# Weights of the seven-product units begin 64 bytes into places that grow by 256 bytes

## The chip, the cores and the metric

The kernel runs on one core of a Trainium2 chip. Five engines work side by side on one on-chip memory of 128 partitions (SBUF): TensorE (PE, with its weight loads shown apart as PEld), VectorE (DVE), ScalarE (ACT), GpSimd (POOL) and SyncE (SP), and DMA queues bring weights in from DRAM. The metric is the device time of one execution in microseconds. Of the kernel before it is 1582.96 us, the median of three runs from 1582.42 to 1583.38.

## The reference

One layer of a decoder trunk: a SwiGLU block, a mixer of two gated linear recurrences, and a second SwiGLU block, for 512 tokens of width 1024, in float32.

```python
D_MODEL = 1024
SEQ = 512
D_FF = 2816

def swiglu(x, w_in, w_out):
    a, b = jnp.split(x @ w_in, 2, axis=-1)
    return (jax.nn.silu(a) * b) @ w_out
...
        h = h + 0.5 * swiglu(rmsnorm(h, ffn1_norm[l]), ffn1_w_in[l], ffn1_w_out[l])
        h = h + hybrid_mixer(rmsnorm(h, mix_norm[l]), w_in[l], lb_all[l], hgrn_out_norm[l],
                             gdn_conv_w[l], gdn_a_log[l], gdn_dt_bias[l], gdn_out_norm[l],
                             w_branch_hgrn[l], w_branch_gdn[l], w_out[l])
        h = h + 0.5 * swiglu(rmsnorm(h, ffn2_norm[l]), ffn2_w_in[l], ffn2_w_out[l])
    return rmsnorm(h, final_norm)
```

The change lies in the products `x @ w_in` of both SwiGLU blocks. Each is a product of a 512 by 1024 matrix with a 1024 by 5632 one.

## The kernel before

**Products in three parts.** Every large product is made of two-part numbers. A weight tile of 128 x 512 is brought into SBUF in float32, ScalarE rounds it into a tile `whi` of the type float32r, and VectorE subtracts to get the rest, `wlo`. The other operand has such a pair, too (`uh`, `ul`, or slices of `xs`). `mm3` (lines 193 to 196) then issues three matmuls: high by high, high by low, low by high. Each matmul has a stationary operand of 128 x 128, which a weight load (LDWEIGHTS) of its own brings into the array, and a moving operand, whose columns stream through. The load of one matmul runs beside the matmul ahead of it.

**Places for weights.** `pair` (line 177) hands out the tiles `wlo` and `whi`. There are two lanes, `w` and `v`, with WB // 2 = 3 places for each of the two tiles, so 12 places of 128 x 512 numbers in all, 2,048 bytes in each partition. The built program puts the first at byte 72,704 of a partition, a multiple of 512, and the others right behind it, so each begins at a multiple of 512. All users of weights share these places: the plain units, the mixer's slabs, and the units below. In SBUF the mixer's tiles and those of the two SwiGLU blocks lie behind them. The operands `uh`, `ul` and `xs` begin at multiples of 512, too.

**Seven-product units.** In a SwiGLU block, `ffn` walks over 22 groups of 2 x 128 columns of `w_in`. The first few are taken as plain products (`plain`), the others by `fast` (line 358), which replaces eight block products by seven products of sums and differences of blocks. There are 17 such groups in the first block and 19 in the second. One group makes seven `Unit`s, each with four blocks of 128 rows, and for each of these `mm3` with 256 columns: 36 x 7 x 4 x 3 = 3024 matmuls, which the profile names px. `xs` holds the seven moving operands. A unit's weight is a loaded tile (`rw`) or a sum or difference of such tiles (`sw`, made by VectorE in line 370).

**Order.** `stream` (line 286) runs through all units of a block in a fixed order. Behind each unit's matmuls, `ahead` prepares weights of later units, up to LEAD = 9 ahead: it asks `pair` for two tiles in the unit's lane, ScalarE writes `whi` (line 333), and VectorE writes `wlo` (line 312). A unit that has a `fold` gets its `wlo` another way: ScalarE writes `-whi` into it (line 337), and a DMA from the POOL queue adds the raw weight from DRAM to that (line 338).

**The other stages.** The blocks' second products (`w_out`) and the mixer use matmuls of 512 columns (pmm, pnat). In pnat the weights are the moving operand, in pmm the stationary one. The order of all instructions is written out by the program, in the mixer by the planner `Desk`.

Of the kernel before, what the change touches and what calls it, by code (L numbers as in the profile page):

```python
# [9 lines left out]
F32R = mybir.dt.float32r  # L10
# [6 lines left out]
P = 128  # L17
# [22 lines left out]
WB = 6  # L40
# [14 lines left out]
LAG = dict(raw=3.5, gb=6.5, nb=6, m=7, out=5.5, back=6, turn=5.5)  # L55
EASE = 2.5
TURNED = (0, 1)
LANES = {"a": 2, "b": 2, "d": 1, "e": 1}


# [85 lines left out]
def body(tc, xT, cst, sqc, hmask, dta, w1o, w1a, w2a, wt, wn, wab, wbh, wbg, wo, w1b, w2b, gfin, y, dbg=None):  # L146
# [4 lines left out]
    wp = ctx.enter_context(tc.tile_pool(name="wp", bufs=1))  # L151
# [22 lines left out]

    taken = [0]

    def pair(lane=None):

        taken[0] += 1
        n = "wv"[taken[0] % 2 if lane is None else lane]  # L180
        return [wp.tile([P, 512], F32R, tag=n + x, name="w" + x, bufs=WB // 2) for x in ("lo", "hi")]

    def slab(src):
        f = src.shape[-1]
# [73 lines left out]
    class Raw:  # L258

        def __init__(self, src, readers=1, fast=False):  # L260
            self.src, self.left, self.fast = src, readers, fast

    class Unit:

        def __init__(self, raws, operand, run, comb=None, drop=(), fold=None, lane=None):
            self.raws, self.operand, self.run, self.comb, self.drop, self.fold = raws, operand, run, comb, drop, fold
            self.lane = lane

    def plain(src, nk, xs, where, n=T, fold=False, roomy=lambda k: False):

# [15 lines left out]
    def stream(units, fp, early, hooks, posts):  # L286

        waiting = [r for u in units for r in u.raws]
        sent = {False: [], True: []}
        for i, u in enumerate(units):  # L290
            u.lane = i % 2 if u.lane is None else u.lane
        lanes = [[i for i, u in enumerate(units) if u.lane == l] for l in range(2)]
        done, combs, parts, fresh = [0, 0], [0], [None] * len(units), []
        room = [99]

        def loads():
            while waiting and room[0]:
                r = waiting[0]
                n = sent[r.fast]
                m = RW if r.fast else RB  # L300
                if len(n) >= m and n[-m].left:
                    break
                r.tile = fp.tile([P, T], F32, name="rw", bufs=RW) if r.fast else \
                    wp.tile([P, T], F32, tag="raw", name="raw", bufs=RB)
                sp.dma_start(r.tile[:, :r.src.shape[-1]], r.src)
                n.append(waiting.pop(0))
                room[0] -= 1

        def ahead(t, most):
            for i in fresh:  # L310
                x, hi, lo = parts[i]
                dve.tensor_tensor(lo, x, hi.bitcast(F32), op=ALU.subtract)  # L312
                for r in units[i].drop:
                    r.left -= 1
            fresh.clear()
            room[0] = 2
            loads()
            while combs[0] < min(t + COMB, len(units)) and not any(r in waiting for r in units[combs[0]].raws):
                if units[combs[0]].comb:
                    units[combs[0]].comb()  # L320
                    loads()
                combs[0] += 1
            for l in (1, 0):
                for _ in range(most):
                    m = done[l]
                    i = lanes[l][m] if m < len(lanes[l]) else len(units)
                    if i >= min(t + LEAD, len(units)) or i >= combs[0] and units[i].fold is None or \
                            any(r in waiting for r in units[i].raws) or m >= WB // 2 and lanes[l][m - WB // 2] > t:
                        break
                    x = units[i].operand()  # L330
                    f = x.shape[-1]
                    lo, hi = (y[:, :f] for y in pair(l))
                    act.copy(hi, x)  # L333
                    parts[i] = x, hi, lo
                    if units[i].fold is not None:

                        act.mul(lo, hi.bitcast(F32), -1.0)  # L337
                        pool.dma_start(lo, units[i].fold, accum_op=ALU.add)  # L338
                        for r in units[i].drop:
                            r.left -= 1  # L340
                    else:
                        fresh.append(i)
                    done[l] += 1
            loads()
        loads()
        for i in range(early):
            ahead(-1, 1)
        for t, u in enumerate(units):
            for f in hooks.get(t, ()):
                f()  # L350
            assert parts[t] and t not in fresh, t
            u.run(*parts[t][1:])
            for f in posts.get(t, ()):
                f()
            ahead(t, 2)
        assert not waiting

    def fast(w, p, xo, fp, at, posts, gate):

        src = lambda n, q: w[ORDER[p], n][:, q * 512:(q + 1) * 512]
        a11, a21, a22, a12 = (Raw(src(*x), r, True) for x, r in (((0, 0), 3), ((1, 0), 2), ((1, 1), 2), ((0, 1), 2)))
        v, one = {}, (slice(0, 256), slice(256, 512))

        def comb(n, x, y, op):
            def f():
                a, b = (z.tile if isinstance(z, Raw) else v[z] for z in (x, y))
                v[n] = fp.tile([P, T], F32, name="sw", bufs=SW)
                dve.tensor_tensor(v[n], a, b, op=op)  # L370
                for z in (x, y):
                    if isinstance(z, Raw):
                        z.left -= 1
            return f

        def prod(o, c, new=None):
            def run(hi, lo):
                if new:
                    v["pt"] = psc.tile([P, T], F32, tag="p" + new, name="px", bufs=LANES[new]) if new != "m" else \
                        psd.tile([P, T], F32, tag="mm", name="px")  # L380
                for i in range(4):
                    k = slice(i * P, (i + 1) * P)
                    mm3(v["pt"][:, one[c]], hi[:, k], lo[:, k], xo[o][0][:, i], xo[o][1][:, i], i == 0, i == 3)
            return run

        def sums(n, add, twice=False):
            t, pt = fp.tile([P, T], F32, name=n, bufs=2 if n == "fa" else 1), v["pt"]
            t2, p2, add = (x.rearrange("p (a t) -> p a t", t=256) for x in (t, pt, add))
            dve.tensor_tensor(t2, p2, add.to_broadcast([P, 2, 256]) if twice else add, op=ALU.add)
            return t  # L390

        def f0():
            v["p1"] = fp.tile([P, 256], F32, name="p1", bufs=2)
            act.copy(v["p1"], v["pt"][:, one[0]])

        def f2():
            v["ua"] = sums("fa", v["p1"], True)

        def f3():
            act.activation(v["ua"][:, one[1]], v["ua"][:, one[1]], AF.Silu)  # L400

        def f4():
            v["uu"] = sums("uu", v["ua"][:, one[0]], True)
            v["vb"] = fp.tile([P, 256], F32, name="vb", bufs=2)
            dve.tensor_tensor(v["vb"], v["pt"][:, one[1]], v["uu"][:, one[0]], op=ALU.add)

        def f6():
            v["uc"] = sums("uc", v["uu"])

        def f7():  # L410
            act.activation(v["uc"][:, one[1]], v["uc"][:, one[1]], AF.Silu)

        def f8():
            ua, uc = v["ua"], v["uc"]
            gate(p, (ua[:, one[1]], uc[:, one[1]]), (uc[:, one[0]], v["vb"]))
        for t, f in ((0, f0), (2, f2), (3, f3), (4, f4), (6, f6), (7, f7), (8, f8)):
            posts.setdefault(at + t, []).append(f)
        raw = lambda x: lambda: x.tile
        of = lambda n: lambda: v[n]
        s1, s2 = comb("s1", a21, a22, ALU.add), comb("s2", "s1", a11, ALU.subtract)  # L420
        return [
            Unit([a11, a21], raw(a11), prod(0, 0, "m"), drop=(a11,), fold=a11.src, lane=1),
            Unit([a22, a12], of("s2"), prod(2, 0, "a"), lane=0, comb=lambda: (s1(), s2())),
            Unit([], raw(a12), prod(3, 1), drop=(a12,), fold=a12.src, lane=1),
            Unit([], of("s1"), prod(1, 1, "b"), lane=0),
            Unit([], of("s3"), prod(4, 0), lane=0, comb=comb("s3", a11, a21, ALU.subtract)),
            Unit([], of("s4"), prod(5, 1, "m"), lane=0, comb=comb("s4", a12, "s2", ALU.subtract)),
            Unit([], raw(a22), prod(6, 0), drop=(a22,), fold=a22.src if 15 <= p < KF - 1 or p < 7 else None, lane=1)]

    def operands(c0, xs, rooms, start, hooks):  # L430

# [1689 lines left out]
```

## Time and profile before

| what | from the page |
|---|---|
| median of three runs | 1582.96 us |
| span of the profiled execution (first to last instruction) | 1579.9 us |
| PE busy | 1570.9 us, 99% |
| weight loads busy | 1359.8 us, 86% |
| DVE, ACT, POOL busy | 72%, 53%, 25% |
| mean granted TensorE clock | 0.999 |
| px matmuls | 3 x 1008, of 128 x 256 |
| DMA | 231.74 MB, mean 147 GB/s |

The profiled execution's own time is not listed apart from its span; the runs lie about 3 us above the span. In the profile a row gives line, engine, operation, "out<-in", the count after an x, then busy time and the mean length of one record in ns. A matmul's record is longer than the distance to the next one, since matmuls overlap in the array. In time, the first SwiGLU block's px stage runs from 62 to 234 us, its second product up to about 355 us, the mixer up to 1227 us, and the second block's px stage from 1273 to 1453 us.

### The profile page before, as it was taken

The page shows a single profiled execution, that of the slowest core. Times are in us where ns is not written, and L with a number is a line of the kernel's source. Part 1 is how long each engine was busy: PE and PEld are TensorE (multiplying, and loading weights), DVE is VectorE, ACT ScalarE, POOL GpSimd, SP SyncE. Part 2 cuts the span into 40 slices and gives each one's busy share as a digit, 9 for nine tenths or more (in the row PEclk, how much of TensorE's full clock was granted, in tenths as well). Part 3 has the DMA queues.
Part 4 walks back from the last instruction along what each step waited for, and adds up shares of the span by engine and source line. Part 5 has one row for each costly group of instructions (what it writes and reads, how often), then busy time and mean ns, then how long its engine had stood idle before and what let it go on. Part 6 is the DMA issues. An engine that isn't in the chain of part 4 may idle for free.

```text
span 1579.9 us, 28718 instructions
## 1 busy us (share of the span) xinstructions
PE 1570.9 (99%) x10388; PEld 1359.8 (86%) x10388; DVE 1130.9 (72%) x2190; ACT 844.0 (53%) x1893; POOL 394.9 (25%) x713
## 2 busy tenths in 40 slices
PE   9999999999999999999999999999999999999998
PEld 8999998888888888888888888888888899999886
DVE  6888786437776778668888887765544799878323
ACT  5666664335354255556676676554324566666322
POOL 0211212000221212436534656430001121121000
PEclk9999999999999999999999999999999999999999
DMA  5767873332313123664464665557544597786431
GB/s 193 169 160 158 174 171 98 108 119 94 107 42 101 52 84 108 193 180 146 137 200 125 194 205 185 176 171 225 154 148 127 142 204 181 175 181 181 137 110 53
DMA packets 155645, 231.74 MB, mean 147 GB/s; under 512 B 22880, under 2 KB 53728, under 8 KB 155504
## 3 DMA queue, kind: packets, MB, share of 16 engines
q1 hardware_dynamic: 138512, 199.63, 40.9%
q0 software_dynamic: 14112, 25.70, 10.4%
q10 hardware_dynamic: 2880, 4.59, 1.0%
q8 instruction: 81, 1.33, 0.3%
q14 instruction: 60, 0.49, 0.1%
HBM read 200.73 MB, written 29.13 MB: 145 GB/s over the span
## 4 chain that ended last, share of the span: by engine, by line
PE 91%; DVE 3%; DMA 2%; issue 2%; ACT 1%; POOL 0%; POOLq 0%; ACTq 0%; DVEq 0%
PE pmm L194 17%; PE pmm L196 17%; PE pmm L195 17%; PE px L196 6%; PE px L195 6%; PE px L194 6%; PE pnat L194 4%; PE pnat L196 4%; PE pnat L195 4%; DMA wlo<-w1b 2%; PE pog L1527 1%; PE pw L1511 1%; PE pgq L1319 1%; PE pl L1066 1%; PE pd L1009 1%
## 5 line engine op out<-in xcount | busy, mean ns | idle before, releaser
L194 PE MATMUL pmm<-uh,whi 128*128 128x512 f32 x830 | 342.7, 413 | 0.3 <-ACT tg L1625 0.2
L196 PE MATMUL pmm<-uh,wlo 128*128 128x512 f32 x830 | 325.0, 392 | 0.0
L195 PE MATMUL pmm<-ul,whi 128*128 128x512 f32 x830 | 324.4, 391 | 0.0
L196 PE MATMUL px<-xs,wlo 128*128 128x256 f32 x1008 | 286.2, 284 | 1.3 <-DMA wlo<-w1b 1.1
L194 PE MATMUL px<-xs,whi 128*128 128x256 f32 x1008 | 285.7, 283 | 0.0
L195 PE MATMUL px<-xs,whi 128*128 128x256 f32 x1008 | 285.6, 283 | 0.0
L1892 DVE TENSOR_TENSOR wlo<-raw,whi 128x512 fp32r<-128x512 f32 x226 | 159.3, 711 | 90.3 <-ACT whi L1890 87.0
L1890 ACT CAST whi<-raw 128x512 fp32r<-128x512 f32 x226 | 139.0, 619 | 130.4 <-PE pmm L195 96.2
L196 PEld LDWEIGHTS px<-xs,wlo 128*128 128x128 f32 x1008 | 193.8, 192 | 2.3 <-DMA wlo<-w1b 1.5
L195 PEld LDWEIGHTS px<-xs,whi 128*128 128x128 f32 x1008 | 193.8, 192 | 0.1
L194 PEld LDWEIGHTS px<-xs,whi 128*128 128x128 f32 x1008 | 193.8, 192 | 0.1
L196 PEld LDWEIGHTS pmm<-uh,wlo 128*128 128x128 f32 x830 | 155.9, 188 | 34.0
L194 PEld LDWEIGHTS pmm<-uh,whi 128*128 128x128 f32 x830 | 156.3, 188 | 31.1 <-ACT tg L1625 0.6
L195 PEld LDWEIGHTS pmm<-ul,whi 128*128 128x128 f32 x830 | 156.5, 189 | 28.5 <-DVE ul L1591 0.4
L333 ACT CAST whi<-sw 128x512 fp32r<-128x512 f32 x144 | 87.6, 613 | 93.5 <-DVE sw L370 72.8
L333 ACT CAST whi<-rw 128x512 fp32r<-128x512 f32 x153 | 94.2, 617 | 72.5 <-PE pnat L196 42.7
L312 DVE TENSOR_TENSOR wlo<-sw,whi 128x512 fp32r<-128x512 f32 x144 | 98.4, 684 | 0.0
L333 ACT CAST whi<-raw 128x512 fp32r<-128x512 f32 x71 | 42.5, 602 | 93.0 <-PE pmm L195 40.3
L1370 POOL TENSOR_TENSOR fm<-gfs,gln 128x60 f32<-128x60 f32 (+24 forms) x155 | 63.2, 408 | 92.9 <-DMA raw<-wt 29.5
L312 DVE TENSOR_TENSOR wlo<-raw,whi 128x512 fp32r<-128x512 f32 x67 | 51.1, 778 | 48.5 <-ACT whi L333 48.5
L338 POOL DMA_DIRECT2D wlo<-w1b x52 | 45.0, 865 | 163.2 <-ACT wlo L337 98.5
L338 POOL DMA_DIRECT2D wlo<-w1a x46 | 39.9, 868 | 154.1 <-ACT wlo L337 123.0
(493 smaller groups left out, 3297.5 us busy)
## 6 DMA issues: line engine op xcount, KB each, us to landing
raw<-wt SPq DMA_DIRECT2D x160, 256.0 KB
rw<-w1b SPq DMA_DIRECT2D x80, 256.0 KB
rw<-w1a SPq DMA_DIRECT2D x74, 256.0 KB
wlo<-w1b POOLq DMA_DIRECT2D x52, 256.0 KB, 5.2
wlo<-w1a POOLq DMA_DIRECT2D x46, 256.0 KB, 5.1
raw<-w2a SPq DMA_DIRECT2D x36, 256.0 KB
raw<-wn SPq DMA_DIRECT2D x32, 256.0 KB
raw<-wbg SPq DMA_DIRECT2D x32, 256.0 KB
```

The costliest lines, as they stand in the source:

```text
L194: pe.matmul(pt, ah, bh, start=first, stop=False)
L195: pe.matmul(pt, ah, bl, start=False, stop=False)
L196: pe.matmul(pt, al, bh, start=False, stop=last)
L312: dve.tensor_tensor(lo, x, hi.bitcast(F32), op=ALU.subtract)
L333: act.copy(hi, x)
L338: pool.dma_start(lo, units[i].fold, accum_op=ALU.add)
L1009: pe.matmul(pd[c // 2][:, (c % 2) * 192:(c % 2) * 192 + 192], ke[:, c * P:(c + 1) * P], qq[:, c], start=True, stop=True)
L1066: pe.matmul(pl_[s0:s0 + 32, c * 16:(c + 1) * 16], ke[:, c * P + s0:c * P + s0 + 32], qv[:, c, r, :, 1], start=True, stop=True)
L1319: pe.matmul(pq[:, (c % 2) * 256:(c % 2) * 256 + 256], kq[:, c, 0], kq[:, c].rearrange("p a b -> p (a b)"), start=True, stop=True)
L1370: pool.tensor_tensor(tv, bc(m[:, j + 1:, j], w), t[:, j:j + 1, :w].to_broadcast([P, n, w]), op=ALU.mult)
L1890: act.copy(hi, raw)
L1892: dve.tensor_tensor(lo, raw, hi.bitcast(F32), op=ALU.subtract)
```

## The change

A constant SHIFT = 16 is added. `pair` takes an offset `off` in numbers. It allocates places of 576 numbers in place of 512 and returns the 512 numbers from `off` on. A `Unit` carries an offset, 0 by default; `fast` sets it to SHIFT, 16 numbers or 64 bytes, for all its seven units, and `ahead` passes it on. The matmuls, the copies, the subtractions and the folding DMA of these units then read and write the shifted part of the place. All other users of `pair` have the offset 0.

```diff
+SHIFT = 16
...
-    def pair(lane=None):
+    def pair(lane=None, off=0):
 
         taken[0] += 1
         n = "wv"[taken[0] % 2 if lane is None else lane]
-        return [wp.tile([P, 512], F32R, tag=n + x, name="w" + x, bufs=WB // 2) for x in ("lo", "hi")]
+        return [wp.tile([P, 576], F32R, tag=n + x, name="w" + x, bufs=WB // 2)[:, off:off + 512] for x in ("lo", "hi")]
...
-        def __init__(self, raws, operand, run, comb=None, drop=(), fold=None, lane=None):
+        def __init__(self, raws, operand, run, comb=None, drop=(), fold=None, lane=None, off=0):
             self.raws, self.operand, self.run, self.comb, self.drop, self.fold = raws, operand, run, comb, drop, fold
-            self.lane = lane
+            self.lane, self.off = lane, off
...
-                    lo, hi = (y[:, :f] for y in pair(l))
+                    lo, hi = (y[:, :f] for y in pair(l, units[i].off))
...
-        return [
+        us = [
             Unit([a11, a21], raw(a11), prod(0, 0, "m"), drop=(a11,), fold=a11.src, lane=1),
...
             Unit([], raw(a22), prod(6, 0), drop=(a22,), fold=a22.src if 15 <= p < KF - 1 or p < 7 else None, lane=1)]
+        for u in us:
+            u.off = SHIFT
+        return us
```

In the built programs the order of the instructions and their waits are the same on every engine; what differs is where tiles lie. The twelve places begin 2,304 bytes after each other, so they begin in turn at a multiple of 512 and 256 bytes past one. In each pair one of `wlo` and `whi` is at the former and the other at the latter. Everything behind the places moves up by 12 x 256 = 3,072 bytes, a multiple of 512.

## The prediction

> **What bounds the kernel now.** The page comes first: its totals by engine, the granted clock, and the chain of work that ended last.
>
> ```profile
> span 1579.9 us, 28718 instructions
> PE 1570.9 (99%) x10388; PEld 1359.8 (86%) x10388; DVE 1130.9 (72%) x2190; ACT 844.0 (53%) x1893; POOL 394.9 (25%) x713
> PEclk9999999999999999999999999999999999999999
> PE 91%; DVE 3%; DMA 2%; issue 2%; ACT 1%; POOL 0%; POOLq 0%; ACTq 0%; DVEq 0%
> L196 PE MATMUL px<-xs,wlo 128*128 128x256 f32 x1008 | 286.2, 284 | 1.3 <-DMA wlo<-w1b 1.1
> L194 PE MATMUL px<-xs,whi 128*128 128x256 f32 x1008 | 285.7, 283 | 0.0
> L195 PE MATMUL px<-xs,whi 128*128 128x256 f32 x1008 | 285.6, 283 | 0.0
> ```
>
> TensorE is never short of work: 91% of the chain is PE, at full clock. The px rows are the products of the seven-product units, 3 x 1008 = 3024 matmuls of 256 columns. The 283 ns is the length of one record; records overlap, so the time that a px matmul really takes is the distance from one start to the next. The windows view gives it: the stretches at 80 to 215 us and at 1290 to 1340 us hold px alone, the one at 270 to 310 us holds matmuls of 512 columns alone.
>
> ```profile
> core 0: us, PE busy (x) PEld busy (x) DVE busy (x) ACT busy (x) POOL busy (x), PEclk, DMA share, GB/s
> 80.00:130.00 50.00, 50.00 (x419) 50.00 (x418) 42.06 (x76) 30.48 (x61) 8.62 (x10) 1.00 0.70 159
> 130.00:180.00 50.00, 50.00 (x419) 50.00 (x419) 41.35 (x73) 31.82 (x62) 10.39 (x12) 1.00 0.77 166
> 180.00:215.00 35.00, 35.00 (x294) 35.00 (x293) 29.55 (x52) 23.91 (x46) 7.76 (x9) 1.00 0.86 178
> 270.00:310.00 40.00, 40.00 (x178) 33.17 (x177) 14.62 (x20) 11.79 (x20) 2.64 (x2) 1.00 0.39 122
> 1290.00:1340.00 50.00, 50.00 (x419) 50.00 (x418) 46.69 (x80) 31.19 (x61) 9.51 (x11) 1.00 0.81 190
> ```
>
> A window counts every record that touches it, so its length plus one record, divided by the count, is the distance between starts. For px that is (50 + 0.283) us / 419 = 120.0 ns, and 35.283 / 294 = 120.0 ns. For 512 columns, with a record of 0.39 us, it is 40.39 / 178 = 226.9 ns. So 256 columns more cost 106.9 ns, and both sizes carry the same remainder: 120.0 - 106.9 = 13.1 ns a matmul that is not the streaming of columns. The px stage as a whole is 3024 x 120.0 ns = 363 us, 23% of the span. Those 13.1 ns x 3024 = 39.6 us are all that a better place for px weights could give on TensorE.
>
> **The change part by part.** No instruction is added, removed or moved, on any engine, and no wait is changed: the two programs differ in addresses alone. So there are three terms.
>
> (1) TensorE reads the px weights, its stationary operand, from 64 bytes past a multiple of 256; before, weights and moving operand both began at multiples of 512. What decides is whether the 13.1 ns is a collision between the read of the moving operand and the weight load that runs beside it. The timeline of TensorE, its matmuls and then its weight loads, has a test: the four-matmul spread at line 247, whose weights are one number per partition, broadcast.
>
> ```profile
> 1230.60 0.39 PE L194 MATMUL pmm<-uh,whi 128*128 128x512 f32 x1
> 1230.83 0.39 PE L195 MATMUL pmm<-ul,whi 128*128 128x512 f32 x1
> 1231.06 0.39 PE L196 MATMUL pmm<-uh,wlo 128*128 128x512 f32 x1
> 1231.28 1.05 PE L247 MATMUL pbc<-sq,rcol 128*128 128x128 f32 x8
> 1231.06 1.08 PEld L247 LDWEIGHTS pbc<-sq,rcol 128*128 128x128 f32 x8
> ...
> 26.19 0.40 PE L196 MATMUL pmm<-uh,wlo 128*128 128x512 f32 x1
> 26.42 1.05 PE L247 MATMUL pbc<-sq,rcol 128*128 128x128 f32 x8
> ...
> 361.53 0.39 PE L196 MATMUL pmm<-uh,wlo 128*128 128x512 f32 x1
> 361.76 1.05 PE L1992 MATMUL pbc<-sq,rcol 128*128 128x128 f32 x8
> ```
>
> The loads of L247 start at 1231.06, together with the matmul L196. Beside L194 and L195 runs a load that sweeps 512 bytes of each partition; beside L196 runs one that stays on a single address. The distances between starts are 0.23, 0.23 and 0.22 us. The other two places with such a spread (line 1992 is the mixer's) have 0.23 and 0.23 us. Without 13.1 ns these three would be 0.214. Three samples, read to 0.01 us, are few, but they say that little or none of the remainder hangs on which addresses the load sweeps. The windows say a second thing against collisions: DMA share goes from 0.70 to 0.86 and VectorE's busy time from 41.4 to 46.7 us in 50, and the px distance stays at 120.0 ns. A memory in which readers stop each other would show such traffic. And the load itself hardly varies:
>
> ```profile
> L196 PEld LDWEIGHTS px<-xs,wlo x1008: 187/192/193, 62.2 to 1452.6; 128*128 128x128 f32 x168
> L247 PEld LDWEIGHTS pbc<-sq,rcol x16: 187/190/193, 26.2 to 1232.0; 128*128 128x128 f32 x16
> ```
>
> No row shows a matmul of this type with an operand that begins off a multiple of 512, so the term is bounded from both sides. The best case is that px falls to the pace of the weight loads. The chain of waits shows that pace where the matmuls are short:
>
> ```profile
> 1226.88 1.68 PE pst L241 x16
> 1231.45 0.89 PE pbc L247 x8
> ```
>
> That is 0.89 / 8 = 111 ns (105 ns at L241, whose matmuls have one column); the nearer row in columns is the 111. So at most 120 - 111 = 9 ns x 3024 = 27 us are gained. The worst case is worked out under the second rival: 13 us lost. I take 0, since the broadcast row is the nearest to a test.
>
> (2) The same 64 bytes hold for the writers of px weights: ScalarE's copy, VectorE's subtraction, and the fold, a DMA that adds into wlo. Engines do not mind: in the seven-product stage of the first block sw begins at multiples of 512, in that of the second block 96 bytes past one, and the subtraction out of it takes 684 ns in both (first row 62 to 234 us, second row 1273 to 1470 us):
>
> ```profile
> L312 DVE TENSOR_TENSOR wlo<-sw,whi 128x512 fp32r<-128x512 f32 x66 | 45.1, 684 | 0.0
> L312 DVE TENSOR_TENSOR wlo<-sw,whi 128x512 fp32r<-128x512 f32 x69 | 47.2, 684 | 0.0
> ```
>
> This is a read; the writes at 64 I take to be as free. For the fold, I compare the plain loads, by the queue's share of 16 engines in a window: 90 to 210 us, where rw begins 32 bytes past a multiple of 512, and 290 to 350 us, where raw begins on one. The other rows are a fold's time from issue to landing, and how long px waited for folds in each block.
>
> ```profile
> q1 hardware_dynamic: 6912, 12.59, 35.9%
> q1 hardware_dynamic: 4085, 6.90, 36.6%
> wlo<-w1b POOLq DMA_DIRECT2D x52, 256.0 KB, 5.2
>   DMA wlo<-w1b: 2.5, 4
>   DMA wlo<-w1a: 0.5, 2
> ```
>
> A packet takes 0.359 x 16 x 120 us / 6912 = 100 ns at 32 bytes and 0.366 x 16 x 60 / 4085 = 86 ns on the boundary, and the first stretch has folds beside it, which slow them. So 16% is the upper bound of what a shifted start costs, 0 the lower; of a fold's 5.2 us that is up to 0.8 us. The cover is the lead with which folds are issued: six waits, 3.0 us in all, exceed it now. Six waits that each grow by 0.8 us make 5 us; my value is 0.5 us.
>
> The Trainium skill speaks against the change here: "DMA: Bandwidth & Descriptors", section "How a descriptor splits into AXI transactions", says that a transfer which does not start on 256 bytes begins at the boundary below it. By it, 2,048 bytes from 64 on would take 66 beats for 64, an estimated 3%, which would make this term about 1 us in place of 0.5. The rows above do not contradict it, and cannot show it.
>
> (3) The places grow from 2,048 to 2,304 bytes, so that every other one now starts 256 bytes past a multiple of 512, and one of the two weights of each pair does so in all other stages, too. All other tiles move up by 12 x 256 = 3,072 bytes, six times 512. By the argument of (1), 0; if 256 matters, it is the third rival.
>
> Sum: 0 + 0.5 + 0 us on the span of 1579.9. What lies around the span is 1582.96 - 1579.9 = 3.1 us, which nothing touches. I predict 1583.4 us.
>
> **The rivals.** (A) The remainder is a collision after all, and a shift of 64 bytes ends it. For it: both reads start together in every px matmul (as the load of L247 and the matmul L196 do at 1231.06) at addresses that agree up to 512, so a collision would be as rigid as what the windows show. Against it: the broadcast row. It would give up to 27 us, 1556 us, and half of it, 1570 us, if one of two collisions goes. The Trainium skill, "TensorE: Matmul & The Clock Gate", section "Back-to-back issue gap", counts 262 cycles, about 109 ns, for 256 columns; the measured 120.0 differs, and by the page's figure an estimated 33 us would be there to gain, though it names no address as the cause.
>
> (B) Slower: a weight load that starts at 64 always crosses a 512-byte boundary, which it never did. Its place is the pace of the loads, 111 ns, which hides behind px's 120.0 and decides once it rises by more than 9 ns. If opening a second block costs what opening a matmul costs, 13.1 ns, the pace is 124.1 ns: 4.1 x 3024 = 12.4 us, and 1595 us. For it: the slack is small and no row has a load off its boundary. Against it: loads take 187 to 193 ns whatever runs beside them.
>
> (C) The change does not do what it says: the other weights do not stay where they were, since half of their places start 256 bytes off. The page's rows for pmm out of uh and ul alone are 830 x 3 = 2490 matmuls of 512 columns; each ns on half of them is 1.2 us. Either sign; 11 ns, the whole remainder but for 2, would be 14 us.
>
> **How the numbers follow.** No change 0.47: the sum. Rival A 0.27, with 0.04 for the good side of C: faster 0.31. Rival B 0.14, longer folds 0.04, the bad side of C 0.04: slower 0.22. The bound of 0.2%, 3.2 us, is about what a measurement of this kernel can tell from no change. The range goes from the bound of A, 1556, to just short of B's price, 1594, and leaves out what is beyond. Alone, the case of no change reaches from 1580 to 1587.
>
> **What would show it.** Right: 419 px records in 50 us again, 178 of 512 columns in 40 us. Rival A shows as up to 453 in 50 us with px loads closer together; rival B as 405, with longer load records; rival C as another count than 178 in the stage of 512 columns; the folds as longer landings than 5.2 us and waits of PE for wlo above 3 us. A px distance off 120.0 ns by over 1 ns makes the prediction wrong.

## The result, and the profile after

The changed kernel takes 1570.07 us, median of five runs from 1570.02 to 1574.84; the kernel before, 1582.96 us, from 1582.15 to 1583.38. The ratio is 0.993, with a 95% interval of 0.9918 to 0.9942, so the change is clear of the noise: 12.9 us lie between the medians and 11.3 us between the means. No change was forecast, so the forecast was wrong. The time agrees with the 1570 us that rival A named for half of its gain, but, as shown below, not for the reason given there.

The page of the profile after, in the lines that answer to those of before:

```profile
span 1567.8 us, 28718 instructions
PE 1558.6 (99%) x10388; PEld 1345.6 (86%) x10388; DVE 1130.0 (72%) x2190; ACT 844.6 (54%) x1893; POOL 397.0 (25%) x713
PE 87%; DMA 5%; issue 4%; DVE 2%; ACT 1%; POOL 0%; POOLq 0%; ACTq 0%; DVEq 0%
```

The span is 12.1 us shorter and PE is busy for 12.3 us less, its weight loads (PEld) for 14.2 us less, and no other engine's busy time moved by 1% (lines of the code are one higher for `mm3`, L195 to L197 in place of L194 to L196). Waits for DMA took 5% of the chain in place of 2%. Where the time went is read from the rows of px, here the first of its matmuls, before and after:

```profile
L194 PE MATMUL px<-xs,whi x1008: 278/283/284, 62.0 to 1452.5; 128*128 128x256 f32 x168
```

```profile
L195 PE MATMUL px<-xs,whi x1008: 276/276/288, 61.9 to 1440.4; 128*128 128x256 f32 x168
```

From the first px matmul of the first block to the last of the second are 1390.5 us before and 1378.5 us after. These 12.0 us are the whole gain. The windows view puts them into the px stages, and leaves the stage of 512 columns between them as it was:

```profile
80.00:130.00 50.00, 50.00 (x427) 50.00 (x426) 42.97 (x77) 30.89 (x60) 8.63 (x10) 1.00 0.73 160
270.00:310.00 40.00, 40.00 (x178) 33.15 (x177) 16.50 (x21) 12.86 (x23) 3.93 (x3) 1.00 0.35 109
1290.00:1340.00 50.00, 50.00 (x443) 50.00 (x443) 49.25 (x83) 33.26 (x64) 9.49 (x11) 1.00 0.82 196
```

With a record of 0.28 us the px distance is 50.28 / 427 = 117.8 ns in the first block and 50.28 / 443 = 113.5 ns in the second, against 120.0 before. So one shift gives two distances. The timeline of TensorE in the first block shows how the one goes over into the other:

```profile
179.19 0.28 PE L195 MATMUL px<-xs,whi 128*128 128x256 f32 x1
179.31 0.28 PE L196 MATMUL px<-xs,whi 128*128 128x256 f32 x1
179.75 0.39 PE L197 MATMUL px<-xs,wlo 128*128 128x256 f32 x1 [0.16 <-DMA wlo<-w1a]
```

TensorE stalls for a fold at 179.3 us. Some matmuls later the distance is 113 ns, where it had been 118 ns for 117 us, from the start of the stage on:

```profile
130.00:175.00 45.00, 45.00 (x385) 45.00 (x384) 38.68 (x69) 29.35 (x57) 9.22 (x11) 1.00 0.73 169
185.00:195.00 10.00, 10.00 (x91) 10.00 (x90) 7.08 (x13) 7.18 (x14) 2.66 (x4) 1.00 0.84 167
```

That is 45.28 / 385 = 117.6 ns and 10.28 / 91 = 113.0 ns, at the same addresses. The px matmuls run in a rhythm that lasts, and a change of rhythm stands behind a stall of TensorE here. A stall need not change it: from 190 to 230 us TensorE stalls in five more places and stays at 113 ns.

### The profile page after: what moved, and what is told of

It reads as the page before. It is cut to its first block, busy times and chain, and to the rows that moved or that the text cites. A ratio compares the mean times of both kernels' runs of the same rounds, so it can differ in the third digit from the quotient of the medians.

```text
span 1567.8 us, 28718 instructions
## 1 busy us (share of the span) xinstructions
PE 1558.6 (99%) x10388; PEld 1345.6 (86%) x10388; DVE 1130.0 (72%) x2190; ACT 844.6 (54%) x1893; POOL 397.0 (25%) x713
## 3 DMA queue, kind: packets, MB, share of 16 engines
q0 software_dynamic: 14112, 25.70, 10.3%
## 4 chain that ended last, share of the span: by engine, by line
PE 87%; DMA 5%; issue 4%; DVE 2%; ACT 1%; POOL 0%; POOLq 0%; ACTq 0%; DVEq 0%
PE pmm L195 17%; PE pmm L196 17%; PE pmm L197 17%; PE px L197 5%; PE px L195 4%; PE px L196 4%; PE pnat L195 4%; PE pnat L197 4%; PE pnat L196 4%; DMA wlo<-w1b 3%; DMA wlo<-w1a 1%; PE pog L1531 1%; PE pw L1515 1%; PE pgq L1323 1%; PE pl L1070 1%
## 5 line engine op out<-in xcount | busy, mean ns | idle before, releaser
L195 PE MATMUL pmm<-uh,whi 128*128 128x512 f32 x830 | 342.4, 413 | 0.3 <-ACT tg L1629 0.2
L197 PE MATMUL pmm<-uh,wlo 128*128 128x512 f32 x830 | 324.7, 391 | 0.0
L196 PE MATMUL pmm<-ul,whi 128*128 128x512 f32 x830 | 324.1, 390 | 0.0
L197 PE MATMUL px<-xs,wlo 128*128 128x256 f32 x1008 | 281.9, 280 | 1.2 <-DVE wlo L313 0.4
L195 PE MATMUL px<-xs,whi 128*128 128x256 f32 x1008 | 280.6, 278 | 0.0
L196 PE MATMUL px<-xs,whi 128*128 128x256 f32 x1008 | 280.6, 278 | 0.0
L197 PEld LDWEIGHTS px<-xs,wlo 128*128 128x128 f32 x1008 | 189.4, 188 | 3.2 <-DVE wlo L313 1.7
L196 PEld LDWEIGHTS px<-xs,whi 128*128 128x128 f32 x1008 | 190.8, 189 | 0.1
L195 PEld LDWEIGHTS px<-xs,whi 128*128 128x128 f32 x1008 | 189.4, 188 | 0.1
L197 PEld LDWEIGHTS pmm<-uh,wlo 128*128 128x128 f32 x830 | 155.8, 188 | 34.2
L195 PEld LDWEIGHTS pmm<-uh,whi 128*128 128x128 f32 x830 | 156.1, 188 | 31.2 <-ACT tg L1629 0.6
L196 PEld LDWEIGHTS pmm<-ul,whi 128*128 128x128 f32 x830 | 156.3, 188 | 28.6 <-DVE ul L1595 0.4
```

The costliest lines, as they stand in the source:

```text
L195: pe.matmul(pt, ah, bh, start=first, stop=False)
L196: pe.matmul(pt, ah, bl, start=False, stop=False)
L197: pe.matmul(pt, al, bh, start=False, stop=last)
```

## The experiments

Theory 1: what counts is where a px weight begins relative to its moving operand. Theory 2: what counts is where the weight load itself begins. Theory 3, formed after the first scans: at 64 bytes there are two rhythms, and a stall decides which of them holds. Each run is set beside the kernel before on the same chip (1581 to 1582 us). The three versions under "Which rhythm" were timed four or five times each, all other experiments once.

**Growth alone.**

```diff
-SHIFT = 16
+SHIFT = 0
```

> The places grow by 256 bytes, but no weight is shifted (offset 0 for all). Theory 1 (what counts is where a px weight begins relative to its moving operand): 256 bytes change nothing, the px distance is 120.0 ns and the time within 2 us of the kernel before. Theory 2 (what counts is that the weight load itself begins off a boundary of 512 bytes): half of the places are off it, so the px distance lies between 113 and 120 ns and about half of the 12.9 us is gained. Rival (the growth alone did it, the other tiles having moved): the whole 12.9 us are gained.

1581.66 us, with 1581.68 before. In the windows px stands at 419 records in 50 us, 120.0 ns, although half of the places begin 256 bytes past a multiple of 512:

```profile
80.00:130.00 50.00, 50.00 (x419) 50.00 (x419) 42.06 (x76) 30.68 (x60) 8.63 (x10) 1.00 0.68 159
```

So the growth by 256 bytes does nothing, for px and for the others (178 matmuls of 512 columns from 270 to 310 us, as before), and theory 2 in its form with 512 bytes falls.

**Both operands shifted, and the moving one alone.** The first is made from the changed kernel, the second from the kernel before.

```diff
-            xs = fp.tile([P, 28, T], F32R, name="xs")
+            xs = fp.tile([P, 28 * T + 16], F32R, name="xs")[:, 16:].rearrange("p (k t) -> p k t", t=T)
```

> The changed kernel with the px moving operands (xs) begun 64 bytes later, too, so that weights and moving operands begin alike again. Theory 1 (relative start): the gain is gone, px distance 120.0 ns, about 1583 us. Theory 2 (the load's own start): the gain stays, 113 to 118 ns, about 1570 us.

> The kernel before with only the px moving operands (xs) begun 64 bytes later; weights and their places as before. Theory 1 (relative start, either sign): the px distance falls below 120 ns, to about 113 to 118 ns if the sign does not matter. Theory 2 (the load's own start): 120.0 ns, no change within 2 us.

With both shifted, px is back at 120.0 ns, first row; with the moving operand alone shifted, at 117.8 ns, second row:

```profile
80.00:130.00 50.00, 50.00 (x419) 50.00 (x418) 42.05 (x76) 30.48 (x60) 8.62 (x10) 1.00 0.70 159
```

```profile
80.00:130.00 50.00, 50.00 (x427) 50.00 (x426) 42.96 (x77) 30.89 (x60) 8.62 (x10) 1.00 0.72 162
```

Theory 1 holds: the weights lie where they lie in the changed kernel in one case and where they lay before in the other, and the distance follows their start relative to xs. In the run with the moving operand alone shifted, px, too, has a second rhythm: by the starts in the timeline it stands at 113.3 ns from 1416 to 1434 us, behind a stall. The times are 1585.52 and 1580.39 us, the first worse than expected by some 3 us and the second short of its px gain. The rest is in the blocks' second products, which use xs again with weights at offset 0. The windows of 512 columns at 1480 to 1530 us, before and with both shifted:

```profile
1480.00:1530.00 50.00, 50.00 (x223) 41.41 (x222) 16.20 (x25) 14.93 (x25) 0.00 (x0) 1.00 0.45 132
```

```profile
1480.00:1530.00 50.00, 50.00 (x216) 40.11 (x215) 16.10 (x24) 13.88 (x24) 0.00 (x0) 1.00 0.43 129
```

50.39 / 223 = 226.0 ns against 50.39 / 216 = 233.3 ns: matmuls of 512 columns get slower by a shift that makes those of 256 faster.

**All weights shifted.**

```diff
-    def pair(lane=None, off=0):
+    def pair(lane=None, off=SHIFT):
...
-        def __init__(self, raws, operand, run, comb=None, drop=(), fold=None, lane=None, off=0):
+        def __init__(self, raws, operand, run, comb=None, drop=(), fold=None, lane=None, off=SHIFT):
```

> The changed kernel with every weight, of all units and of the mixer, begun 64 bytes into its place. Theory 1 (relative start counts for every matmul): px as in the changed kernel, 113 to 118 ns. For 512 columns the runs with shifted xs showed 233 ns where the stationary operand begins 64 bytes past the moving one (227 ns when both begin alike) and 228 to 230 ns where the moving one does: some 3,500 matmuls x 6 ns = 21 us slower, some 740 x 2 ns = 1.5 us slower, against 12 us gained, so 10 to 12 us slower than before, about 1592 us. Rival (those 233 ns came from waits in that stage, not from the start): 227 ns, about 1570 us.

1591.48 us, 10.3 us slower than before, as worked out. At 512 columns the distance is 40.39 / 173 = 233.5 ns. In this run px went at 113.2 ns in the first block from its start on, where the changed kernel had 117.8: the same px addresses, another rhythm. One change of rhythm in this run speaks against theory 3: at 207.9 us, where a new group of units begins, px goes over from 113 to 118 ns, and no distance near there is above 120 ns.

```profile
80.00:130.00 50.00, 50.00 (x444) 50.00 (x443) 44.82 (x80) 31.94 (x62) 8.63 (x10) 1.00 0.74 167
270.00:310.00 40.00, 40.00 (x173) 32.08 (x172) 16.12 (x21) 12.70 (x22) 3.92 (x3) 1.00 0.33 103
```

**Places that grow by 64 bytes.**

```diff
-        return [wp.tile([P, 576], F32R, tag=n + x, name="w" + x, bufs=WB // 2)[:, off:off + 512] for x in ("lo", "hi")]
+        return [wp.tile([P, 528], F32R, tag=n + x, name="w" + x, bufs=WB // 2)[:, off:off + 512] for x in ("lo", "hi")]
```

> The changed kernel with places that grow by 64 bytes only (528 numbers), so that places begin 0, 64, 128 and 192 bytes past multiples of 256 in turn, for all users. Theory 1: the matmuls of 512 columns lose their common start, three quarters of them run at 229 to 233 ns, some 3 to 4 ns x 4,300 on average, 13 to 17 us, and px units stand at all four distances, about 117.5 ns on average, 7 us gained: 5 to 10 us slower than before. Rival (only the shift inside the place counts): about 1570 us.

1589.83 us, 8.3 us slower than before. The rows have 50.28 / 428 = 117.5 ns for px and 40.39 / 175 = 230.8 ns for 512 columns, both as expected. The growth by 256 bytes thus does no good by itself, but this smaller one costs the other stages more than px gains.

```profile
80.00:130.00 50.00, 50.00 (x428) 50.00 (x428) 42.87 (x76) 31.42 (x61) 8.65 (x10) 1.00 0.72 162
270.00:310.00 40.00, 40.00 (x175) 32.63 (x174) 15.10 (x20) 12.18 (x21) 2.63 (x2) 1.00 0.36 109
```

**Scans of the offset.** One kernel gives each group of seven-product units its own offset (two groups in a row for most values); a second does the same with finer steps; a third shifts the weights of the 512-column products.

```diff
-SHIFT = 16
+SCAN = (5, (0, 0, 4, 4, 8, 8, 12, 12, 16, 16, 32, 32, 48, 48, 64, 64, 0)), (3, (64, 56, 56, 48, 40, 40, 32, 28, 28, 24, 24, 20, 20, 16, 12, 8, 4, 2, 2))
...
-            u.off = SHIFT
+            u.off = SCAN[w is w1b][1][p - SCAN[w is w1b][0]]
```

In the third, `Unit` gets the offsets of the second products:

```diff
-                                roomy=lambda k, d=d: d < 2 and k % 8 == 4)
+                                roomy=lambda k, d=d: d < 2 and k % 8 == 4, off=(0, 4, 8, 12, 16, 32, 48, 56)[d])
...
-            return Unit([raw], lambda: raw.tile, run, drop=(raw,))
+            return Unit([raw], lambda: raw.tile, run, drop=(raw,), off=(0, 4, 8, 12, 16, 24, 32, 40, 48, 56, 0)[p // 2])
```

> Places as in the changed kernel, but each group of seven-product units has an offset of its own, 0 to 64 numbers (0 to 256 bytes). Theory 1 and theory 2 alike: groups at 0 run at 120.0 ns, groups at 16 numbers at 113 to 118 ns; a meeting of two reads that is merely put off should vary smoothly with the offset and come back to 120 ns at 64 numbers (256 bytes) if the memory's pattern repeats by then; if only the first bytes matter, every offset over some size gives the same 113 to 118 ns. In sum 5 to 12 us faster than before.

> The changed kernel with finer offsets for the groups of seven-product units: near 64 bytes (52, 56, 60, 64, 68, 72, 76), small ones (4, 8, 12, 24) and near 256 (208 to 252). Theory 1 with a meeting that depends on lines of 16 bytes: 60 behaves as 48, 68 to 76 as 64 (113 to 118 ns). If single words count, the distance differs from word to word. Offsets of 4 and 8 bytes: 118 to 120 ns.

> The changed kernel; in addition the weights of the first block's second product (stationary, 512 columns) begin 0, 16, 32, 48, 64, 128, 192 and 224 bytes into their places, one value for each of its eight column groups, and those of the second block's second product (moving, 512 columns) 0, 16, 32, 48, 64, 96, 128, 160, 192, 224 and 0 bytes, one for every two of its row groups. Theory 1: 227 ns at 0 in both, 233 ns at 64 bytes in the first, 228 to 230 ns at 64 in the second; some other value might fall below 227, down to 216, if a meeting of two reads makes all of what 512 columns take beyond their streaming. Rival (that remainder is no meeting): no value below 226 ns.

Distances in ns, from starts inside the groups (a count in a short window can be off by one, which is 4 ns in 14 us of 512 columns):

```
px, offset in bytes     0   8   16   32   48   60   64   68   72   76   80  112  160  192  224  256
distance              120 116  118  118  118  119  113  118  118  113  120  120  120  118  117  120
512 columns, stationary weight, offset   16   32   48   64  128  192  224
distance                                227  233  233  233  232  229  233
512 columns, moving weight, offset       16   32   48   64   96  128  160  192  224
distance                                232  233  233  229  234  233  234  233  233
```

At 16 bytes px has 118 in the first block and 120 in the second. The px offsets left out of the table, 4, 12, 24, 40, 56, 96, 128, 144, 176, 208, 216, 232, 240, 244, 248 and 252 bytes, lie between 117 and 120, so 64 and 76 bytes alone reached 113. The value at 0 of the 512 columns is 226.9. The distance comes back to 120 at 256 bytes and is not smooth in the offset, so a meeting that is merely put off does not explain it. Single words seem to count: 72 and 80 bytes show 118 and 120 where 76 shows 113, against the lines of 16 bytes that the expectation named. That is not shown beyond doubt, since an offset can have a faster rhythm than the one its groups were in. Two rows of the fine scan, at 72 and at 76 bytes, show the step (19.28 / 163 = 118 ns, 9.28 / 82 = 113 ns):

```profile
132.00:151.00 19.00, 19.00 (x163) 19.00 (x162) 16.10 (x29) 11.68 (x23) 3.45 (x4) 1.00 0.74 166
151.50:160.50 9.00, 9.00 (x82) 9.00 (x81) 7.85 (x15) 5.92 (x12) 1.72 (x2) 1.00 0.72 167
```

For px a common start was among the worst cases, and for 512 columns no offset is better than it. No px value is below 113, and no 512-column value below 226. The table says what was found in these groups, not what an offset always gives: 64 bytes has 113 here and 118 in most of the changed kernel's first block. Of the expected values, 8 bytes lies outside, with 116 and not 118 to 120, and 60 bytes does not behave as 48 (119 and 118). The times, 1577.10, 1576.44 and 1577.00 us, mix all this; they are 4 to 5 us below those of before, where 5 to 12 were expected of the first.

**Which rhythm.** The changed kernel again, one with another offset in the first group of each block, and one at 76 bytes, side by side and repeated:

```diff
-            u.off = SHIFT
+            u.off = 12 if p == (3 if w is w1b else 5) else SHIFT
```

```diff
-SHIFT = 16
+SHIFT = 19
```

> The changed kernel again, as the measure for the two that run beside it: 12 to 13 us faster than before. Theory 3 (at 64 bytes px has two rhythms, 117.8 and 113.3 ns, and a stall of TensorE decides which of them holds until the next stall): both rhythms appear again, changing at waits alone, perhaps at other places than in the first profile.

> The changed kernel, but the first group of seven-product units of each block begins 48 bytes into its places, all others 64. In the scan the group behind one at 48 bytes ran at 113.3 ns. Theory 3: both blocks enter the fast rhythm behind the first group and keep it until the first stall: px 2 to 5 us shorter than in the changed kernel, less what stalls take back. Rival (the rhythm comes from the traffic of the stage, not from where it was entered): 117.8 ns in the same groups as in the changed kernel, and no change beyond 1 us.

> All px weights begin 76 bytes into their places, not 64. In the fine scan the one group at 76 bytes ran at 113.3 ns. Theory 3 with two rhythms here, too: 113.3 and some slower one, the time within 3 us of the changed kernel. If 76 bytes has the fast rhythm alone: all groups at 113.3 ns but for waits, px 4 to 6 us shorter, about 6 us faster than the changed kernel at best.

The changed kernel has 1575.51 us here (1572.76 to 1576.12; ratio to before 0.9957, interval 0.9942 to 0.9972), 5 us more than in the first comparison, and 6 us less than before where 12 to 13 were expected. Its profile shows where: the stretch of the second block that ran at 113.5 ns there runs at 50.28 / 427 = 117.8 ns here:

```profile
1290.00:1340.00 50.00, 50.00 (x427) 50.00 (x426) 47.73 (x81) 31.54 (x62) 8.65 (x10) 1.00 0.81 194
```

Counted by the starts in the timelines, about 2,100 px matmuls are in the slow rhythm here and about 1,380 in the first profile, which is 720 x 4.5 ns = 3.2 us. The waits of px for weights are 7.3 us here and 4.1 us there, 3.2 us more. Together they cover the 5.5 us between the two profiled spans (1573.3 and 1567.8 us).

The other entry gave 1571.57 us (0.9937, 0.9921 to 0.9952), but not for the reason expected: the first block stayed at 117.8 ns in its window (427 records in 50 us). The second changed several times, with the fast rhythm, 15.28 / 135 = 113.2 ns, in this stretch:

```profile
1310.00:1325.00 15.00, 15.00 (x135) 15.00 (x134) 14.86 (x25) 9.50 (x18) 3.46 (x4) 1.00 0.80 175
```

So the offset of the entry does not choose the rhythm by itself, and the expectation was a miss. At 76 bytes the time is 1566.29 us (1565.53 to 1569.44; ratio 0.9908, 0.9892 to 0.9923), with 113 ns in both blocks:

```profile
80.00:130.00 50.00, 50.00 (x444) 50.00 (x443) 44.85 (x80) 32.60 (x62) 8.65 (x10) 1.00 0.73 165
1290.00:1340.00 50.00, 50.00 (x442) 49.86 (x441) 49.33 (x86) 31.88 (x62) 8.65 (x10) 1.00 0.83 195
```

Neither window shows the slow rhythm, and by the starts in the timeline none of the 36 groups does, though px waits for weights 17 times here and 15 times in the changed kernel's first profile. This version beats both kernels: 15 us faster than before, 9 us than the changed one beside it, more than the 6 us that the expectation held possible.

**A load that stays on one address.** Made from the kernel before:

```diff
-                    mm3(v["pt"][:, one[c]], hi[:, k], lo[:, k], xo[o][0][:, i], xo[o][1][:, i], i == 0, i == 3)
+                    hb, lb = (z[:, i * P:i * P + 1].to_broadcast([P, P]) for z in (hi, lo))
+                    mm3(v["pt"][:, one[c]], hb, lb, xo[o][0][:, i], xo[o][1][:, i], i == 0, i == 3)
```

> The kernel before, but each px weight load reads one column of its 128 and broadcasts it, so that it stays on one address of each partition and does not sweep 512 bytes; the seven products of the units are then other sums than the reference's (127 of 128 weight columns are left out). Everything else, starts included, is as before. Theory 1 with a meeting of two sweeping reads: nothing is met, px falls to 111 to 114 ns, the time by 15 to 25 us. Rival (the prediction's reading of the broadcast row: what the load reads does not matter): 120.0 ns, within 2 us of the kernel before. Third outcome (a load that stays on one address meets the other read in another way): some other distance, above 114 and not 120.

1577.09 us, with 1582.08 before. The third outcome came for the most part: 50.28 / 431 = 116.7 ns in most of the first block, 120.0 ns in most of the second. Between the two, behind a stall in each block, px also runs at 113 ns, for 26 and 20 us, here 16.78 / 148 = 113.4 ns (second row).

```profile
80.00:130.00 50.00, 50.00 (x431) 50.00 (x431) 43.42 (x78) 30.88 (x60) 8.63 (x10) 1.00 0.73 163
171.50:188.00 16.50, 16.50 (x148) 16.50 (x148) 12.68 (x24) 11.66 (x23) 5.19 (x6) 1.00 0.90 191
1290.00:1340.00 50.00, 50.00 (x419) 50.00 (x418) 47.22 (x80) 30.47 (x61) 8.51 (x10) 1.00 0.78 188
```

A load that stays on one address can hold px at 120.0 ns, too. So what meets is not two sweeps that run over the same bytes; and an unchanged distance beside a broadcast load says nothing against a meeting. The run settles another question, too. ScalarE, VectorE and the folds write the weights, so their writes move with every shift of the weights; here, as in the run with xs alone shifted, these writes are as before, and the distance changes all the same. Here only what the load reads differs.

## Why the prediction was wrong, step by step

- **Where the kernel is bound:** right. All of the gain is on PE in the px stages, and the distance between px starts was the number to look at.
- **The remainder of 13.1 ns in both sizes: failed.** It took the difference of the two distances, 106.9 ns, for the streaming of 256 columns, as if both sizes carried the same extra. The runs show the extra to be the sizes' own: 512 columns are at their lowest with a common start, 226.9 ns, and px was far from its lowest. Half of 226.9 is 113.5, and no run has px below 113, so at their lowest both sizes take the same time per column, 0.443 ns, with nothing left that goes by the matmul. Down to that lowest value 120.0 - 113.4 = 6.6 ns x 3024 = 20 us were to be had. The rows of before held a hint of it: per column, 120.0 / 256 = 0.469 ns against 226.9 / 512 = 0.443. They could not say which of the two readings is right.
- **"I take 0, since the broadcast row is the nearest to a test": this is the step that decided, and it failed.** The row stood beside a matmul of 512 columns, the size at which no start found is better than the common one, so no gain could show there. And the run with broadcast loads in px shows that such a load can leave 120.0 ns in place.
- **The steady 120.0 ns under changing traffic, taken as evidence against collisions: failed.** The 117.8 ns of the changed kernel, which hang on where the weights begin, hold as steadily for 117 us. That the distance moves with the start of weights relative to xs, goes back to 120.0 when both move, and changes with what the load alone reads, shows that it depends on how the two operands' reads lie to each other. Whether they collide in the memory is not shown.
- **Folds:** right. Their median landing is 5.1 us where it was 5.2, and 2.0 us of waits for them (1.2 and 0.8) stand where 3.0 did. The estimated 3% by the Trainium skill, "DMA: Bandwidth & Descriptors", section "How a descriptor splits into AXI transactions", is not seen in them.
- **The growth by 256 bytes:** right, by the run with the growth alone.
- **Rival A:** right that the start of the px weights is worth time, and mis-sized in price: its floor was taken as the 111 ns of the loads, 27 us, and the lowest distance is 113.4 ns, 20 us. Of these the profile after gives 12.0. That this meets its half price, 1570 us, is luck: not half of a loss went in every matmul, but a little over half of the matmuls gained some 6.6 ns and the others 2.2, and a second comparison gave 1575.51 us. The kernel at 76 bytes shows where the rest can go. Its first px row runs from 62.0 to 1436.8 us, 15.7 us less than before, and its px idled as follows:

```profile
  DVE wlo L313: 3.5, 9
  DMA wlo<-w1a: 2.7, 5
  DMA wlo<-w1b: 1.3, 3
```

That is 7.5 us of waits for weights, 4.2 us more than the 3.3 of before (0.3 for VectorE and 3.0 for folds); 15.7 + 4.2 = 19.9 us, the 20 us again. In the changed kernel these waits come to 4.1 us, 0.8 more, so some 7 us are left. The slow rhythm takes most of them: about 1,380 of the 3,024 matmuls, a little under half, at 4.4 ns each are 6.1 us; the rest lies in longer distances right behind stalls.
- **Rival B, loads that cross a boundary:** fell. Loads at 64 bytes have a median of 188 ns, 4 less than before.

## What to carry to other kernels

Compare the distance between matmul starts per column across sizes; a size that is above the others has something to gain even when TensorE is busy for 99% of the time. Then try where the stationary operand begins relative to the moving one, in steps of a word, for each size by itself, since what helps one size can cost another as much. A distance that stays the same under all traffic may be a rhythm that lasts, one of several; look at it again behind stalls, and repeat the timing, since two rhythms give two times for one program.

## What was not expected of the hardware

With the same addresses, px runs at 117.8 or 113.4 ns, and with a broadcast load at 116.7, 113.4 or 120.0 ns, for tens of microseconds and more, with nearly all changes at stalls. Medians of the changed kernel in two comparisons differ by 5.4 us, in good part for that, where those of the kernel before agree to within 1.5 us. What in the memory or in TensorE's sequence makes the rhythms, whether single words count, why 76 bytes found only the fast one, and why a common start suits 512 columns and not 256, stays open: the runs show the dependence, not its cause.
